# Narrow sample matmuls of a recurrent layer padded to full tiles, with elementwise work moved from VectorE to ScalarE

## The chip, the cores and the metric

One core of a Trainium2 chip runs the whole program. The metric is device time in microseconds (us); several executions are made and their median counts. The kernel before takes 676.6 us (three runs, 675.25 to 676.72).

## The reference

Two decoder layers are applied, one after the other, to a prompt of 512 tokens and to a sample group of 8 sequences with 4 new tokens each (32 tokens); the model is 1024 wide and everything is fp32.

Layer 0 projects the normalized input once into attention heads (q, k, v, gate) and convolution channels. Each of 8 heads attends within blocks; the softmax that the change touches is

```python
s = jnp.concatenate([s_sel.reshape(shp[:-2] + (n_sel,)), s_own], axis=-1)
p = jax.nn.softmax(s, axis=-1)
```

A depthwise convolution of length 31 runs beside it, and both go through one output projection.

Layer 1 is a gated linear recurrence with a 128x128 state for each of 8 heads. In chunks it computes

```python
o_inter = jnp.einsum('bhtk,bhkv->bhtv', qc * jnp.exp(b), S)
a = jnp.einsum('bhtk,bhsk,bhtsk->bhts', qc, kc, decay)
o = o_inter + jnp.einsum('bhts,bhsv->bhtv', a, vc)
S = (jnp.exp(b_last)[..., None] * S
     + jnp.einsum('bhsk,bhsv->bhkv', kc * jnp.exp(b_last[:, :, None, :] - b), vc))
```

For the samples each of the 8 sequences has its own state `S0` of 128x128 in each head, which is read, used for the 4 new tokens, updated and written back. After it come a normalization for each head, a gate and the output projection.

## The kernel before, in words

Activations lie transposed: features on the 128 partitions, 544 tokens (512 prompt, 32 sample) along the free axis, in two halves of 272 columns. A projection is a `unit`: eight blocks of the contraction times three matmuls 128x128 by 272 columns (lines 142 to 144; weights and activations are split into a high and a low fp32r part, and three of the four products are taken). The result lies in one of three PSUM buffers tagged `g`; ScalarE or VectorE evicts it. A weight tile is loaded by SyncE's queue (line 130), its high part is made on ScalarE (line 133), its low part on VectorE (line 134). Smaller PSUM buffers are tagged `s` (two), `t` (two) and `o` (one).

Layer 0: `prep` projects q, k, v and the gate of a pair of heads, `attend` takes a block of 128 queries at a time. For each of its two heads a score matmul (lines 470 and 472) fills a buffer, VectorE takes the maximum (478), ScalarE scales it (479) and computes the exponential with its sum (481), VectorE takes the reciprocal (482) and multiplies the 128 to 512 columns by it (483), TensorE transposes the result (line 102, the helper `transpose`), ScalarE copies it out (488), and TensorE multiplies by v (493). There are 32 such steps. Between them VectorE works through the convolution, 120 multiply-adds of 512 columns (line 516).

Layer 1: `proj` projects one head, `scan` runs its recurrence. The change lies in the last third of `scan`. There, for each head: `kk` is transposed (line 102), copied to `ktk` by VectorE (879) and, for the samples, to `kts` by the helper `rep4` (line 704); line 885 multiplies for the prompt's state, which VectorE chains (888, 890); lines 898 and 900 form the prompt's output. The samples' output `pos` is the sum of two matmuls, `as_` by `vs` at line 904 (32 rows by 32 columns of the array) and a selection matrix by `c4` at line 912 (128 rows by 32 columns); between them line 908 multiplies the sample queries by the states, in four column tiles 32 wide, and line 911 copies to `c4`. Line 918 forms the states' update in two halves of 512 columns, and eight VectorE instructions (line 921) scale the old states and add it. Then squares and sums on ScalarE (929, 931), the scaled output on VectorE (935, and 937 for the samples' 32 rows, tile `ons`), five transposes (four of `on` and a 32-row one of `ons`, all at line 102) and the gate (945).

The code gives dependencies, buffers and a few priorities; the order on each engine is made when the program is built, by a scheduler that simulates a timeline (`schedule_with_timeline_sim=True`). It lays `proj` of the next head between the steps of `scan`. The steps of `attend` are raised by `tc.high_priority(offset=300)`. Heads 6 and 7 are run against each other by hand (`drain(s6, s7)`), and the output projection follows in two phases. ScalarE, VectorE and GpSimd carry out their instructions in that built order.

Of the kernel before, what the change touches and what calls it, by code (L numbers as in the profile page):

```python
# [19 lines left out]
TP = 512  # L20
# [11 lines left out]
C_EXP = 448  # L32
C_SEL = 456
C_SEL2 = 472
C_END = 504


def consts():
# [28 lines left out]
def hybrid_step(ctx, tc, xt_in, cache_kt, cache_v, conv_in, hgrn_in, page_table, par_in, k_norm_0,  # L67
# [110 lines left out]
    with tc.tile_pool(name="l0", bufs=1) as lp:  # L178
# [285 lines left out]
        def attend(c, rq, qT, kT, vt, ga):  # L464
            po = bank("o")
            for i in range(4):
                L = 128 * (i + 1)
                ss = [bank("s"), bank("s")]
                for hh in range(2):
                    PE.matmul(ss[hh][:, :L], qT[:, i * 128:(i + 1) * 128], kT[:, hh, 0:L], start=True, stop=False)  # L470
                for hh in range(2):
                    PE.matmul(ss[hh][:, L - 128:L], identb, causb, start=False, stop=True)  # L472
                PTs = []
                for hh in range(2):
                    rqc = rq[:, 2 * i + hh:2 * i + hh + 1]
                    s = ss[hh]
                    mx = mk(lp, "mx", [128, 4], 4)
                    V.tensor_reduce(mx[:, 0:1], s[:, :L], axis=AX.X, op=ALU.max, negate=True)  # L478
                    A.activation(mx[:, 1:2], mx[:, 0:1], AF.Copy, scale=rqc)
                    P = mk(qp, "PP", [128, 512], 3)  # L480
                    A.activation(P[:, :L], s[:, :L], AF.Exp, bias=mx[:, 1:2], scale=rqc, accum_out=mx[:, 2:3])  # L481
                    V.reciprocal(mx[:, 3:4], mx[:, 2:3])
                    V.tensor_scalar_mul(P[:, :L], P[:, :L], mx[:, 3:4])
                    pT = bank("t")
                    for j in range(i + 1):
                        transpose(pT[:, j * 128:(j + 1) * 128], P[:, j * 128:(j + 1) * 128], 128)
                    PT = mk(qp, "PT", [128, 512], 3)
                    A.activation(PT[:, :L], pT[:, :L], AF.Copy)  # L488
                    PTs.append(PT)
                for j in range(i + 1):  # L490
                    for hh in range(2):
                        r = slice(64 * hh, 64 * hh + 64)
                        PE.matmul(po[r, i * 128:(i + 1) * 128], vt[:, j, r],  # L493
                                  PTs[hh][:, j * 128:(j + 1) * 128], start=(j == 0), stop=(j == i),
                                  tile_position=(0, 64 * hh))
            mh, ml = mtile(("h", c)), mtile(("l", c))
            V.scalar_tensor_tensor(ga[:, :TP], po, 0.5, ga[:, :TP], op0=ALU.mult, op1=ALU.mult)
            split(mh[:, :TP], ml[:, :TP], ga[:, :TP])
# [164 lines left out]
    with tc.tile_pool(name="l1", bufs=1) as lp:  # L663
# [14 lines left out]
        V.tensor_tensor(lbm[:, 3], lbm[:, 1], lbm[:, 2], op=ALU.add)  # L678
        V.tensor_tensor(lbm[:, 4], lbm[:, 3], lbm[:, 1], op=ALU.subtract)
        V.tensor_scalar(lbm[:, 5], lbm[:, 4], -1.0, 1.0, op0=ALU.mult, op1=ALU.add)  # L680
        ADs, AT, ADx, QS = [], [], [], []
        for b in range(2):
            ad = lp.tile([128, 4, 32], F32, name=f"AD{b}")
            at = lp.tile([128, 4, 128], F32, name=f"AT{b}")
            as_ = lp.tile([32, 32], F32, name=f"AS{b}")
            qs = lp.tile([128, 2, TS], F32, name=f"QS{b}")
            QS.append(qs)
            for t in (ad, at, as_, qs):
                G.memset(t, 0.0)
            ADs.append(ad)  # L690
            AT.append(at)
            ADx.append(as_)
# [4 lines left out]
        def rep4(out, src, los, n, raw=None):  # L697
            r4 = mk(lp, "r4", [128, 4, TS], 2)
            G.tensor_copy(r4, src[:, TP:T].unsqueeze(1).to_broadcast([128, 4, TS]))
            pv = bank("t", 128)  # L700
            transpose(pv, r4.rearrange("p a t -> p (a t)"), 128)
            if raw is not None:
                V.tensor_copy(raw, pv[:TS])
            A.activation(out, pv, AF.Copy)
            for l in los:
                V.tensor_tensor(out[l:l + n], pv[l:l + n], out[l:l + n], op=ALU.subtract)

        def proj(hd):
# [44 lines left out]
            for i in range(4):  # L753
                transpose(pv[:, i * 128:(i + 1) * 128], vT[:, i * 128:(i + 1) * 128], 128)
            A.activation(vt, pv, AF.Copy)
            vs = mk(lp, "vs", [TS, 128], 2)
            vx = mk(lp, "vx", [128, 128], 2, F32R)
            rep4(vx, vT, (32, 96), 32, vs)
            return f, kk, qx, qq, vt, vs, vx, gg
# [1 line left out]
        def scan(hd, f, kk, qx, qq, vt, vs, vx, gg):  # L761
# [20 lines left out]
            for l in range(4):  # L782
# [1 line left out]
                V.copy_predicated(ad.rearrange("p c (g t) -> p c g t", t=4)[:, :, :, l:],  # L784
                                  m.unsqueeze(1).to_broadcast([128, 4, 8, 4 - l]),
                                  lag(pl[:, :320].rearrange("p (c x) -> p c x", c=4), l))
                V.copy_predicated(as_.rearrange("p (n g t) -> p n g t", n=1, t=4)[:, :, :, l:], m[:32].unsqueeze(1),
                                  lag(pl[:32, 320:400].unsqueeze(1), l))
            for b2 in range(2):
                A.activation(qs[:, b2].rearrange("p (j u t) -> p j u t", u=2, t=4)[:, :, b2],  # L790
# [85 lines left out]
            for c in range(4):  # L876
                transpose(pk[:, c * 128:(c + 1) * 128], kk[:, c * 128:(c + 1) * 128], 128)
            ktk = mk(lp, "ktk", [128, 512], 1)
            V.tensor_copy(ktk, pk)
            kts = mk(lp, "kts", [128, 128], 2, F32R)  # L880
            rep4(kts, kk, (64,), 64)

            psu = bank("t")
# [16 lines left out]
                    PE.matmul(po[:, sl], qq[:, sl], S[:, (c - 1) * 128:c * 128], start=False, stop=True)  # L900
            S0 = mk(lp, "S0", [128, NS, 128], 2)
            SP.dma_start(S0, hgrn_in[hd])
            pos = bank("s", 128)[:TS]
            PE.matmul(pos, as_, vs, start=True, stop=False)
            p4 = bank("t", 128)
            for b2 in range(2):
                for j in range(4):
                    PE.matmul(p4[32 * j:32 * j + 32, :], qs[:, b2], S0[:, 2 * j + b2], start=(b2 == 0), stop=(b2 == 1),
                              tile_position=(0, 32 * j))
            c4 = mk(lp, "c4", [128, 128], 2)  # L910
            A.activation(c4, p4, AF.Copy)
            PE.matmul(pos, cst[:, C_SEL2:C_SEL2 + 32], c4, start=False, stop=True)
            ve = mk(lp, "ve", [128, NS, 128], 1, F32R)
            G.tensor_tensor(ve, vx.unsqueeze(1).to_broadcast([128, NS, 128]),  # L914
                            exm.unsqueeze(2).to_broadcast([128, NS, 128]), op=ALU.mult)
            for g in range(2):
                pn = bank("t")
                PE.matmul(pn, kts, ve[:, 4 * g:4 * g + 4, :].rearrange("p n v -> p (n v)"), start=True, stop=True)  # L918
                for n4 in range(4):
                    n = 4 * g + n4  # L920
                    V.scalar_tensor_tensor(S0[:, n, :], S0[:, n, :], tots[:, n:n + 1], pn[:, n4 * 128:(n4 + 1) * 128],  # L921
                                           op0=ALU.mult, op1=ALU.add)
            SP.dma_start(hgrns_out[hd], S0)
            yield

            sq = mk(lp, "sq", [128, 128], 2)
            sd = mk(lp, "sd", [128, 24], 2)
            G.memset(sd, 1.0)
            A.activation(sq[:TS], pos, AF.Square, accum_out=sd[:TS, 4:5])
            for c in range(4):  # L930
                A.activation(sq, po[:, c * 128:(c + 1) * 128], AF.Square, accum_out=sd[:, c:c + 1])
            rsqrt(sd[:, 8:13], sd[:, 0:5], sd[:, 16:21], 1.0 / 128, V)
            on = mk(lp, "on", [128, 4, 128], 1)
            ons = mk(lp, "ons", [TS, 128], 2)
            V.tensor_tensor(on, po.rearrange("p (c v) -> p c v", c=4), sd[:, 8:12].unsqueeze(2).to_broadcast([128, 4, 128]),
                            op=ALU.mult)
            V.tensor_scalar(ons, pos, sd[:TS, 12:13], None, op0=ALU.mult)
            gn = mk(lp, "gn", [128, T], 1)
            pk = bank("t")
            for c in range(4):  # L940
                transpose(pk[:, c * 128:(c + 1) * 128], on[:, c], 128)
            pks = bank("t", TS)
            transpose(pks, ons, TS)
            for p, sl in ((pk[:, :256], slice(0, 256)), (pk[:, 256:], slice(256, TP)), (pks, slice(TP, T))):
                V.scalar_tensor_tensor(gn[:, sl], p, vec("on"), gg[:, sl], op0=ALU.mult, op1=ALU.mult)
            for sl in (slice(0, 256), slice(256, T)):
                split(oh[hd][:, sl], ol[hd][:, sl], gn[:, sl])
# [82 lines left out]
```

## Time and profile before

| what | value |
|---|---|
| median of three runs | 676.6 us |
| the profiled execution's own time | 673.57 us |
| its span, first to last instruction | 670.7 us |
| mean granted TensorE clock | 0.991 |
| TensorE busy, share of the span | 96% |
| VectorE busy | 81% |
| ScalarE busy | 47% |
| GpSimd busy | 10% |

In the profile PE is TensorE's matmul side and PEld its weight loads, which run beside the matmuls; DVE is VectorE, ACT is ScalarE, POOL is GpSimd. "L912" is line 912. A matmul's duration in the profile runs from its issue to the end of its drain and overlaps the next one's, so what a matmul costs a busy TensorE is the step from its start to the next one's start. A shape such as 128\*32 ahead of a matmul's operands is the part of the array that it uses, rows by columns. The profiled execution lies 3.0 us under the median, and 2.9 us of its time lie around the span.

### The profile page before, as it was taken

To read this page: it belongs to the slowest core of one execution; us is meant where nothing else is said; L and a number is where in the kernel's file an instruction comes from. 1 tells how busy PE (TensorE), PEld (TensorE's weight loads), DVE (VectorE), ACT (ScalarE), POOL (GpSimd) and SP (SyncE) were. 2 spreads that over 40 slices of the span, in tenths; PEclk is the share of its full clock that TensorE was granted. 3 is DMA by queue.
4 is the path that set the end of the run, shared out by engine and by line. 5 is a ranking of instruction groups with operands and counts; after the bars stand their busy time and mean duration, and the time that the engine had idled before them with its cause. 6 is when DMAs were issued, how large, how long until landed. Compare 5 with 4: busy or idle time off the path is not lost.

```text
span 670.7 us, 14828 instructions
## 1 busy us (share of the span) xinstructions
PE 646.7 (96%) x5806; PEld 583.2 (87%) x5806; DVE 541.8 (81%) x1326; ACT 313.8 (47%) x760; POOL 70.1 (10%) x93
## 2 busy tenths in 40 slices
PE   8899999988998999999989999999999999999997
PEld 7799999966877976659989999899989989899997
DVE  6999999899967975646978977878787878777676
ACT  7332444625656867434665435443434343344221
POOL 6000110000111100000001210211011202020100
PEclk9899999989999999999999999999999999999999
DMA  9422343122120151674552232232223222222114
GB/s 254 166 80 64 98 144 108 59 70 63 50 80 31 65 175 41 222 268 143 161 162 93 70 95 100 75 119 80 97 86 122 71 100 81 97 76 83 54 56 145
DMA packets 34583, 70.51 MB, mean 105 GB/s; under 512 B 7378, under 2 KB 16210, under 8 KB 34514
## 3 DMA queue, kind: packets, MB, share of 16 engines
q1 hardware_dynamic: 34514, 69.58, 32.5%
q8 instruction: 45, 0.74, 0.4%
q14 instruction: 24, 0.20, 0.1%
HBM read 59.84 MB, written 9.73 MB: 104 GB/s over the span
## 4 chain that ended last, share of the span: by engine, by line
PE 88%; DVE 6%; DMA 2%; ACT 2%; issue 1%; SPq 1%; DVEq 0%
PE g L142 23%; PE g L144 22%; PE g L143 22%; PE t L102 4%; PE s L470 3%; DVE m L516 2%; PE o L493 2%; PE s L622 1%; PE s L779 1%; PE t L885 1%; DVE wl L134 1%; PE o L898 1%; PE o L900 1%; DMA kn<-in_cache_kt_dram 1%; DMA wr<-in_w_in_dram 1%
## 5 line engine op out<-in xcount | busy, mean ns | idle before, releaser
L142 PE MATMUL g<-h,wh 128*128 128x272 f32 x944 | 277.5, 294 | 9.3 <-ACT ga L247 3.8
L143 PE MATMUL g<-h,wh 128*128 128x272 f32 x944 | 275.6, 292 | 1.7 <-DVE h L273 1.7
L144 PE MATMUL g<-h,wl 128*128 128x272 f32 x944 | 276.0, 293 | 0.0
L142 PEld LDWEIGHTS g<-h,wh 128*128 128x128 f32 x944 | 179.4, 190 | 13.6 <-ACT ga L247 4.5
L143 PEld LDWEIGHTS g<-h,wh 128*128 128x128 f32 x944 | 179.2, 190 | 4.0 <-DVE h L273 2.1
L144 PEld LDWEIGHTS g<-h,wl 128*128 128x128 f32 x944 | 179.3, 190 | 2.0 <-issue 1.2
L133 ACT ACTIVATE wh<-wr 128x1024 fp32r<-128x1024 f32 (+4 forms) x90 | 88.2, 982 | 106.3 <-PE g L143 94.1
L134 DVE TENSOR_TENSOR wl<-wr,wh 128x1024 fp32r<-128x1024 f32 (+4 forms) x90 | 101.0, 1123 | 25.5 <-ACT wh L133 25.2
L516 DVE SCALAR_TENSOR_TENSOR m<-m,vecs,m 128x512 f32<-128x512 f32 x120 | 84.1, 735 | 0.0
L143 PE MATMUL g<-m,wh 128*128 128x272 f32 x256 | 74.2, 292 | 0.0
L144 PE MATMUL g<-m,wl 128*128 128x272 f32 x256 | 73.8, 291 | 0.0
L142 PE MATMUL g<-m,wh 128*128 128x272 f32 x256 | 73.5, 295 | 0.0
L142 PEld LDWEIGHTS g<-m,wh 128*128 128x128 f32 x256 | 47.3, 188 | 6.0 <-issue 3.6
L143 PEld LDWEIGHTS g<-m,wh 128*128 128x128 f32 x256 | 48.2, 188 | 2.5 <-issue 1.0
L144 PEld LDWEIGHTS g<-m,wl 128*128 128x128 f32 x256 | 48.1, 188 | 0.3 <-issue 0.2
L470 PE MATMUL s<-kz,qT 128*128 128x128 f32 (+3 forms) x64 | 23.7, 454 | 1.2 <-ACT PP L481 1.2
L921 DVE SCALAR_TENSOR_TENSOR S<-S,tot,t 128x128 f32<-128x128 f32 x64 | 17.6, 341 | 6.2 <-PE t L918 6.1
L488 ACT ACTIVATE PT<-t 128x128 f32<-128x128 f32 (+3 forms) x32 | 13.8, 434 | 18.7 <-PE t L102 18.7
L478 DVE TENSOR_REDUCE mx<-s 128x1 f32<-128x128 f32 (+3 forms) x32 | 15.4, 482 | 7.6 <-PE s L472 7.1
L863 DVE TENSOR_TENSOR kk<-kk,tot 128x256 f32<-128x256 f32 (+1 forms) x48 | 20.0, 417 | 0.0
L481 ACT ACTIVATE PP<-s,mx,rq 128x128 f32<-128x128 f32 (+3 forms) x32 | 19.7, 616 | 0.5
L914 POOL TENSOR_TENSOR ve<-vx,cst 128x1024 fp32r<-128x1024 f32 x8 | 15.9, 1985 | 37.5 <-PE t L918 17.7
(289 smaller groups left out, 973.0 us busy)
## 6 DMA issues: line engine op xcount, KB each, us to landing
wr<-in_w_in_dram SPq DMA_DIRECT2D x58, 512.0 KB, 3.6
wr<-in_w_out_dram SPq DMA_DIRECT2D x16, 512.0 KB, 3.6
kn<-in_cache_kt_dram SPq DMA_DIRECT2D x16, 256.0 KB, 3.4
kn<-in_cache_v_dram SPq DMA_DIRECT2D x16, 256.0 KB, 3.8
S<-in_hgrn_dram SPq DMA_DIRECT2D x8, 512.0 KB, 3.6
out_hgrns_dram<-S SPq DMA_DIRECT2D x8, 512.0 KB, 2.6
xTall<-in_xt_dram SPq DMA_DIRECT2D x8, 272.0 KB, 5.6
out_y_dram<-xTall SPq DMA_DIRECT2D x8, 272.0 KB, 2.4
```

Of the source, the lines that this page charges most:

```text
L102: PE.transpose(out, in_, ident[:np_, :np_])
L133: A.activation(wh, raw, AF.Copy)
L134: V.tensor_tensor(wl, raw, wh, op=ALU.subtract)
L142: PE.matmul(ps, wh[:, k - k0, :], ah, start=(k == k0), stop=False)
L143: PE.matmul(ps, wh[:, k - k0, :], al, start=False, stop=False)
L144: PE.matmul(ps, wl[:, k - k0, :], ah, start=False, stop=(k == k1 - 1))
L470: PE.matmul(ss[hh][:, :L], qT[:, i * 128:(i + 1) * 128], kT[:, hh, 0:L], start=True, stop=False)
L481: A.activation(P[:, :L], s[:, :L], AF.Exp, bias=mx[:, 1:2], scale=rqc, accum_out=mx[:, 2:3])
L516: V.scalar_tensor_tensor(cy[c][:, :TP], up[c][:, j:j + TP], cw[:, c, j:j + 1], cy[c][:, :TP], op0=ALU.mult, op1=ALU.add)
L863: V.tensor_tensor(k3[:, :, 0, :], k3[:, :, 0, :], t3[:, :, 1:2].to_broadcast([128, nblk, hsz]), op=ALU.mult)
L914: G.tensor_tensor(ve, vx.unsqueeze(1).to_broadcast([128, NS, 128]), exm.unsqueeze(2).to_broadcast([128, NS, 128]), op=ALU.mult)
L921: V.scalar_tensor_tensor(S0[:, n, :], S0[:, n, :], tots[:, n:n + 1], pn[:, n4 * 128:(n4 + 1) * 128], op0=ALU.mult, op1=ALU.add)
```

## The change

The 32x32 tile `AS` and the 32-row tile `vs` become 128x128 tiles that hold zeros beyond the 32 used rows and columns; the selection matrix is widened by 96 zero columns (so the constants grow from 504 to 600 columns); `ons` gets 128 rows. The matmuls at lines 904 and 912 and the fifth transpose thereby use the full array. The samples' states are scaled in place on ScalarE, in eight instructions of 128 columns, and VectorE adds the update in two instructions of 512 columns in place of eight of 128. `ktk` is copied by ScalarE. The buffers of `kts`, `c4` and `ons` go from two to one. In layer 0 the multiplication by the softmax's reciprocal (line 483) goes from VectorE to ScalarE.

```diff
-C_END = 504
+C_END = 600
...
                     V.reciprocal(mx[:, 3:4], mx[:, 2:3])
-                    V.tensor_scalar_mul(P[:, :L], P[:, :L], mx[:, 3:4])
+                    A.activation(P[:, :L], P[:, :L], AF.Copy, scale=mx[:, 3:4])
...
-            as_ = lp.tile([32, 32], F32, name=f"AS{b}")
+            as_ = lp.tile([128, 128], F32, name=f"AS{b}")
+            vs = lp.tile([128, 128], F32, name=f"VS{b}")
+            VS.append(vs)
...
-            for t in (ad, at, as_, qs):
+            for t in (ad, at, as_, qs, vs):
                 G.memset(t, 0.0)
...
-                V.tensor_copy(raw, pv[:TS])
+                V.tensor_copy(raw[:TS], pv[:TS])
...
-            vs = mk(lp, "vs", [TS, 128], 2)
+            vs = VS[hd % 2]
...
-            V.tensor_copy(ktk, pk)
-            kts = mk(lp, "kts", [128, 128], 2, F32R)
+            A.activation(ktk, pk, AF.Copy)
+            kts = mk(lp, "kts", [128, 128], 1, F32R)
...
-            pos = bank("s", 128)[:TS]
+            pos = bank("s", 128)
             PE.matmul(pos, as_, vs, start=True, stop=False)
...
-            c4 = mk(lp, "c4", [128, 128], 2)
+            c4 = mk(lp, "c4", [128, 128], 1)
             A.activation(c4, p4, AF.Copy)
-            PE.matmul(pos, cst[:, C_SEL2:C_SEL2 + 32], c4, start=False, stop=True)
+            PE.matmul(pos, cst[:, C_SEL2:C_SEL2 + 128], c4, start=False, stop=True)
+            for n in range(NS):
+                A.activation(S0[:, n], S0[:, n], AF.Copy, scale=tots[:, n:n + 1])
...
-                for n4 in range(4):
-                    n = 4 * g + n4
-                    V.scalar_tensor_tensor(S0[:, n, :], S0[:, n, :], tots[:, n:n + 1], pn[:, n4 * 128:(n4 + 1) * 128],
-                                           op0=ALU.mult, op1=ALU.add)
+                V.tensor_tensor(S0[:, 4 * g:4 * g + 4], S0[:, 4 * g:4 * g + 4], pn.rearrange("p (n v) -> p n v", n=4),
+                                op=ALU.add)
...
-            A.activation(sq[:TS], pos, AF.Square, accum_out=sd[:TS, 4:5])
+            A.activation(sq, pos, AF.Square, accum_out=sd[:, 4:5])
...
-            ons = mk(lp, "ons", [TS, 128], 2)
+            ons = mk(lp, "ons", [128, 128], 1)
...
-            V.tensor_scalar(ons, pos, sd[:TS, 12:13], None, op0=ALU.mult)
+            V.tensor_scalar(ons, pos, sd[:, 12:13], None, op0=ALU.mult)
...
-            pks = bank("t", TS)
-            transpose(pks, ons, TS)
-            for p, sl in ((pk[:, :256], slice(0, 256)), (pk[:, 256:], slice(256, TP)), (pks, slice(TP, T))):
+            pks = bank("t", 128)
+            transpose(pks, ons, 128)
+            for p, sl in ((pk[:, :256], slice(0, 256)), (pk[:, 256:], slice(256, TP)), (pks[:, :TS], slice(TP, T))):
```

## Rows read from the trace of the kernel before

**Rows 1.** page, part 1: busy us (share of the span) xinstructions

```profile
PE 646.7 (96%) x5806; PEld 583.2 (87%) x5806; DVE 541.8 (81%) x1326; ACT 313.8 (47%) x760; POOL 70.1 (10%) x93
```

**Rows 2.** page, part 4: the chain that ended last, by engine

```profile
PE 88%; DVE 6%; DMA 2%; ACT 2%; issue 1%; SPq 1%; DVEq 0%
```

**Rows 3.** stretches: us, busy PE, PEld, DVE, ACT, POOL, PEclk, DMA share, GB/s

```profile
118.00:205.00 87.00, 79.27 (x572) 68.00 (x571) 76.96 (x157) 45.59 (x103) 5.16 (x2) 0.98 0.20 62
205.00:266.00 61.00, 58.04 (x449) 47.45 (x448) 49.48 (x116) 44.89 (x105) 5.27 (x7) 1.00 0.23 75
350.00:670.00 320.00, 316.85 (x3296) 294.56 (x3296) 249.54 (x760) 127.97 (x374) 38.73 (x46) 0.99 0.28 91
```

**Rows 4.** waits of PE from 350 us on: total us, times, longest

```profile
PE g L142 <- ACT f L713: 2.6, 1, 2.6
```

**Rows 5.** timeline of PE around L912: start us, us, engine line op xcount

```profile
433.00 0.39 PE L898 MATMUL o<-vt,AT 128*128 128x128 f32 x2
433.23 0.39 PE L900 MATMUL o<-S,qq 128*128 128x128 f32 x2
433.54 0.41 PE L912 MATMUL s<-c,cst 128*32 128x128 f32 x2
433.88 0.73 PE L918 MATMUL t<-ve,kts 128*128 128x512 f32 x2
```

**Rows 6.** timeline of PE around L904

```profile
457.20 0.40 PE L904 MATMUL s<-vs,AS 32*32 32x128 f32 x2
...
457.76 0.29 PE L143 MATMUL g<-h,wh 128*128 128x272 f32 x1
```

**Rows 7.** timeline of PE around the transpose of ons

```profile
412.75 0.60 PE L102 MATMUL t<-cst,on 128*128 128x128 f32 x4
413.28 0.24 PE L102 MATMUL t<-cst,ons 32*128 32x32 f32 x1
...
413.68 0.29 PE L143 MATMUL g<-h,wh 128*128 128x272 f32 x1
```

**Rows 8.** timeline of PE, from a full transpose into a unit

```profile
424.61 0.27 PE L102 MATMUL t<-cst,r 128*128 128x128 f32 x1
...
424.85 0.29 PE L144 MATMUL g<-h,wl 128*128 128x272 f32 x1
```

**Rows 9.** weight loads by shape: xcount, busy us, mean ns, idle us before

```profile
L898 PEld LDWEIGHTS o<-vt,AT 128*128 128x128 f32 x64 | 9.2, 191 | 0.0
...
L912 PEld LDWEIGHTS s<-c,cst 128*32 128x32 f32 x16 | 1.1, 108 | 1.0
```

**Rows 10.** VectorE after 370 us, the same columns

```profile
L921 DVE SCALAR_TENSOR_TENSOR S<-S,tot,t 128x128 f32<-128x128 f32 x64 | 17.6, 341 | 6.2 <-PE t L918 6.1
...
L935 DVE TENSOR_TENSOR on<-o,sd 128x512 f32<-128x512 f32 x8 | 5.5, 692 | 0.3
```

**Rows 11.** ScalarE from 100 to 270 us, operations with a scale per partition

```profile
L479 ACT ACTIVATE mx<-mx,rq 128x1 f32<-128x1 f32 x32 | 9.0, 287 | 6.9 <-DVE mx L478 6.7
...
L436 ACT ACTIVATE kz<-t,gq 64x512 f32<-64x512 f32 x8 | 5.4, 679 | 3.9 <-PE t L102 3.8
```

**Rows 12.** L483 in two stretches: us, VectorE's busy us (count)

```profile
118.00:205.00 87.00, 6.20 (x17) 0.98 0.20 62
205.00:266.00 61.00, 6.87 (x15) 1.00 0.23 75
```

**Rows 13.** waits of PE, 100 to 270 us: total us, times, longest

```profile
PE g L142 <- ACT ga L247: 3.8, 2, 2.5
PE o L493 <- ACT PT L488: 1.5, 3, 0.7
...
PE t L102 <- DVE ksT L437: 1.3, 1, 1.3
PE s L470 <- ACT PP L481: 1.2, 3, 0.6
```

**Rows 14.** page, part 5: the convolution's multiply-adds

```profile
L516 DVE SCALAR_TENSOR_TENSOR m<-m,vecs,m 128x512 f32<-128x512 f32 x120 | 84.1, 735 | 0.0
```

More of the change, by code (lines that the diff above doesn't have):

```diff
@@ L680, in hybrid_step @@
         V.tensor_scalar(lbm[:, 5], lbm[:, 4], -1.0, 1.0, op0=ALU.mult, op1=ALU.add)
-        ADs, AT, ADx, QS = [], [], [], []
+        ADs, AT, ADx, QS, VS = [], [], [], [], []
         for b in range(2):
@@ L786, in scan @@
                                   lag(pl[:, :320].rearrange("p (c x) -> p c x", c=4), l))
-                V.copy_predicated(as_.rearrange("p (n g t) -> p n g t", n=1, t=4)[:, :, :, l:], m[:32].unsqueeze(1),
+                V.copy_predicated(as_[:TS, :TS].rearrange("p (n g t) -> p n g t", n=1, t=4)[:, :, :, l:], m[:32].unsqueeze(1),
                                   lag(pl[:32, 320:400].unsqueeze(1), l))
```

## The prediction

> **What bounds the kernel now.** I read four views in this order. The busy shares [rows 1] make TensorE the candidate: 646.7 of 670.7 us. A busy share can hide waits, so the chain that ended last comes next [rows 2]: 88% of it is TensorE, 6% VectorE, 2% ScalarE. Then the stretches [rows 3]: from 350 us on (layer 1) TensorE is busy in 316.85 of 320 us, while VectorE has 249.54 and ScalarE 127.97; from 118 to 205 us (attention beside the convolution) TensorE has 79.27 of 87 us and VectorE 76.96. Last, TensorE's own waits. In the whole of layer 1 there is one that the view lists, 2.6 us at the start, for ScalarE's L713 [rows 4]. So in layer 1 a us taken from VectorE buys nothing, and a us of TensorE's own time buys a us. In layer 0 TensorE waits now and then for either of the other two [rows 13].
>
> **Layer 1, the padded matmuls.** These are the only TensorE instructions that change, and a matmul costs the step from start to start. A pair of full-size fp32 matmuls takes 0.23 us to the next pair (L898 at 433.00, L900 at 433.23) [rows 5]. Into the 32-column pair of L912 the step is 433.54 - 433.23 = 0.31, and out of it into L918 433.88 - 433.54 = 0.34 [rows 5]. Changing the shape of the array in use thus costs 0.08 going in and 0.11 coming out, 0.19 together. The reverse way is the padding: all three groups get the full shape of the work behind them.
>
> L904, the 32x32 pair: from its start to the second matmul of the unit behind it, 457.76 - 457.20 = 0.56 us [rows 6]. I count to the second, because the first one's weights also come late. A full-size transpose takes 424.85 - 424.61 = 0.24 to the same place [rows 8], and a pair has one more step of half of 0.23, so padded it is 0.24 + 0.115 = 0.355, and 0.205 is saved. What stands before it is left out of the sum: where that is a full-size matmul another 0.08 would go.
>
> The transpose of `ons`: the four of `on` begin at 412.75, in steps of half of 0.23, so the last begins at about 413.08; `ons` follows at 413.28 and the second matmul behind it at 413.68 [rows 7]. From the last `on` that is 0.60; padded it is 0.115 + 0.24 = 0.355, and 0.245 is saved.
>
> Sum: 0.19 + 0.205 + 0.245 = 0.64 us in each head, **5.1 us in eight**, all of it in a stretch where TensorE does not wait. The cost side is the weight load: 108 ns for 32 columns, 191 ns for 128 [rows 9], two loads each at L904 and L912. I take nothing for it, since the loads of 191 ns at L898 already stand in the pairs of 0.23 us; if all of it came onto the path it would be 4 x 8 x 0.083 = 2.7 us, and that is one end of the range.
>
> **Layer 1, the work that moves.** VectorE gives up 64 instructions of 0.341 us and gets 16 of about 0.692 (the nearest row, 128x512 from PSUM) [rows 10]: 21.8 - 11.1 = 10.7 us less, and a `t` buffer is held for 0.69 in place of 4 x 0.341 = 1.36 us. TensorE waits for neither now, so the gain is nothing. ScalarE gets 64 scalings of 128 columns. It has no such row; with a scale per partition one column takes 0.287 and 512 take 0.679 [rows 11], which makes 0.38 for 128, 24.6 us in all; `ktk` adds 8 x 0.68 = 5.4 at most. ScalarE goes from 128 to about 158 of 320 us [rows 3]. The cover is its idle 162 us. If that is gone at one place, a burst of 8 x 0.38 = 3.1 us stands in a head ahead of the evictions of `g`, the high weight parts and the squares of L931, and TensorE waits for a `g` buffer; three of them stand against that. The scalings wait for the reads of L908, but `c4` ahead of them on ScalarE already waits for those, so no new wait comes ahead of the queue. `kts`, `c4` and `ons` with one buffer are written once in a head and read before the next head writes them: nothing, and where it fails, the writer waits for L918, L912 or a transpose. The larger zero fills on GpSimd run once, before the first head, and the constants' transfer on SyncE's queue grows by 49 KB, a tenth of one weight tile: nothing for both.
>
> **Layer 0, the division.** VectorE gives up 6.20 us from 118 to 205 us, where it is busy 76.96 of 87, and 6.87 us from 205 to 266 us [rows 3, 12]. ScalarE gets 32 multiplications; by its two rows 128, 256, 384 and 512 columns take 0.38, 0.48, 0.58 and 0.68, eight of each 17.0 us [rows 11], against 13.1 us before. Each step of attention grows by 0.12 us on the mean and gets one more hand-over, from the reciprocal on VectorE to ScalarE. Queued behind that wait on ScalarE are the exponential of the other head, the evictions of `prep` and the next high weight part; transposes at L102, then L488 and L493, wait for its end. The gain is bounded by VectorE's 6.20 us (TensorE is idle for 7.7 us there [rows 3]); the loss is priced below. TensorE waits for PT and PP in six places, 2.7 us, for `ga` 3.8, for `ksT` 1.3 [rows 13]: some of that will shrink with a freer VectorE and some grow with a fuller ScalarE. Between a gain of up to 6.2 and a loss of up to 12.4 I take nothing: the waits that exist are mostly behind ScalarE, which argues against the gain, and in 26 of 32 steps TensorE does not wait at all, which argues against the loss.
>
> A rule speaks against this part. The Trainium skill, "ScalarE: Activation LUTs", section "Rules for kernel authors", sends plain multiplications and additions to VectorE and not ScalarE. By that page's formula with one pointer operand an estimate for the 32 multiplications is 17.5 us, and the sum would not move. The rows agree that ScalarE is the slower of the two here (0.679 [rows 11]); what decides is the queue, in the second rival.
>
> **Sum.** The profiled execution took 673.57 us, its span 670.7; with 5.1 less it would be 668.5. It lies 3.0 us under the median, which I leave as it is: 676.6 - 5.1 = **671.5 us**.
>
> **The rivals.** *VectorE's relief counts.* In the stretch at 118 us both engines are nearly full; if TensorE's waits there shrink by all that VectorE gives up, 6.2 us, the time is 665.3. For it speaks VectorE's 88% in that stretch; against it that the largest wait, 3.8 us for `ga`, ends on ScalarE [rows 13].
>
> *ScalarE waits in line behind the convolution, and the kernel gets slower.* Place: the 17 divisions from 118 to 205 us [rows 12]. The reciprocal stands on VectorE between multiply-adds of 0.735 us [rows 14]; when it is one of them late, ScalarE stands still, and everything queued behind it does. Price: 17 x 0.73 = 12.4 us, which gives 683.9. It decides from the point where 5.1 + 1.4 = 6.5 us come through to TensorE, nine of the 17. Against it: the scheduler can lay other ScalarE work ahead of the multiplication, and ScalarE is busy only 45.59 of 87 us there [rows 3]. A few of these waits, three to eight, give 673.7 to 677.3.
>
> *The padding does not give what it says.* With the weight loads on the path the gain of layer 1 is 5.1 - 2.7 = 2.4, 674.2 us. Against it stand the pairs of 0.23 us.
>
> In the Trainium skill, "TensorE: Matmul & The Clock Gate", section "LDWEIGHTS (loading the stationary operand)", a load costs by its columns and not its rows. By its formula an estimate of this rival's price is 4 x 8 x 80 ns = 2.6 us. The rows' 108 and 191 ns agree with the difference.
>
> **How the numbers follow.** Forecast (669.5 to 673.5, which also allows a rebuilt order to add or drop some eight changes of shape elsewhere): 0.55. VectorE's relief: 0.14. A few waits on ScalarE: 0.14. Nine or more: 0.09. Weight loads: 0.08. A measurement of this kernel can tell about 0.2%, 1.4 us, from no change. Faster by more takes the forecast, the relief, the loads and a quarter of the few waits: 0.81. Within it lies the rest of the few waits: 0.10. Slower is the full queue: 0.09. The range 666 to 677 leaves out the full queue, the top of the few waits and the lowest part of the relief, some 0.15.
>
> **What would show it.** Right: L904, L912 and the `ons` transposes in shape 128\*128, with 0.23 us from the pair of L912 to L918 and 0.24 from `ons` to the second matmul behind it; TensorE's waits after 350 us still a single one of about 2.6 us; VectorE's busy time lower by about 16 us in layer 1 (10.7, and some 5 for `ktk`, by its price on ScalarE) and 13 in layer 0. Wrong: new waits of L102 or L493 for L483 on ScalarE; waits of units for evictions behind the state's scaling; steps over 0.3 us around L912; or a layer 1 that is not shorter by about 5 us from its first unit to the last instruction.

## The result, and the profile after

The changed kernel takes **670.6 us** (median of ten runs, 666.6 to 672.1) against 675.2 us for the kernel before in the same comparison: 0.9932 times, interval [0.9908, 0.9956], which is 4.6 us faster. The prediction was 671.5 us, 5.1 us faster.

The profiled execution took 672.1 us, the longest of its ten runs; that of before took 673.57 us, less than most of its own. So the two spans are nearly equal, 670.3 and 670.7 us, and can't be compared as a whole. Read in two parts they show where the time went. From the first to the last matmul of layer 1 the time falls from 316.6 to **309.6 us**. Layer 1 begins at 356.9 us instead of 349.9.

Page of the kernel after, part 1 (as in [rows 1]) and the engines' shares of the chain that ended last (as in [rows 2]):

```profile
PE 642.5 (96%) x5806; PEld 584.0 (87%) x5806; DVE 519.8 (78%) x1238; ACT 350.9 (52%) x866; POOL 67.5 (10%) x95
...
PE 87%; DVE 6%; DMA 2%; ACT 2%; issue 1%; SPq 1%; POOL 0%; DVEq 0%
```

TensorE has the same 5806 matmuls and 4.2 us less busy time. VectorE lost 22.0 us, ScalarE gained 37.1. Neither of these shows in the chain.

The stretches, columns as in [rows 3], of the kernel after; the rows from 118, 205 and 350 us answer to those:

```profile
100.00:118.00 18.00, 18.00 (x144) 17.46 (x143) 16.51 (x32) 9.16 (x22) 0.00 (x0) 1.00 0.32 104
118.00:205.00 87.00, 78.93 (x574) 68.29 (x573) 72.17 (x142) 51.77 (x115) 2.35 (x2) 0.98 0.20 62
205.00:266.00 61.00, 56.74 (x397) 46.49 (x396) 42.73 (x99) 50.37 (x118) 5.91 (x7) 0.97 0.23 75
266.00:357.00 91.00, 85.59 (x728) 68.33 (x726) 57.72 (x114) 46.88 (x93) 2.15 (x12) 0.98 0.53 177
...
350.00:670.00 320.00, 313.98 (x3329) 297.46 (x3327) 241.88 (x711) 152.76 (x452) 39.79 (x58) 0.99 0.28 93
```

and the same ahead of layer 1 in the kernel before, where the stretches between are in [rows 3]:

```profile
100.00:118.00 18.00, 18.00 (x145) 17.46 (x143) 16.47 (x32) 8.20 (x20) 0.00 (x0) 1.00 0.31 104
...
266.00:350.00 84.00, 79.98 (x677) 64.95 (x676) 56.89 (x111) 42.88 (x84) 1.68 (x10) 1.00 0.60 190
```

From 100 us to the start of layer 1 both kernels issue nearly the same matmuls: the counts of TensorE sum to 1843 in both, where one that runs across the edge of two stretches counts twice. Before, they take 250 us, of which TensorE is busy 235.3; after, 257 us, busy 239.3. The 7.0 us are 3.0 us more idle time and 4.0 us more for the same matmuls, with a granted clock of 0.97 and 0.98 from 205 us on, where it was 1.00. Between 100 and 660 us the clock fell in this execution from 2.4 to its lower level, 1.2 GHz, near 186, 217, 285 and 357 us, each time after TensorE had stood waiting; in that of before near 140 and 351 us. One of these falls in the stretches of the kernel after (columns as above):

```profile
183.00:185.00 2.00, 0.71 (x7) 0.59 (x6) 1.34 (x4) 1.36 (x2) 0.00 (x0) 1.00 0.64 244
185.00:187.00 2.00, 1.51 (x8) 1.24 (x6) 1.76 (x4) 0.40 (x1) 0.00 (x0) 0.70 0.06 19
187.00:189.00 2.00, 2.00 (x11) 2.00 (x10) 1.27 (x2) 0.00 (x0) 0.00 (x0) 0.50 0.44 120
```

TensorE is busy 0.71 of 2 us, then the clock falls to 0.50, and it is full again at half speed. The ten executions of this kernel differ in their mean granted clock, from 0.985 to 0.995, so one pair of profiles can't tell how much of the 7.0 us belongs to the change; runs price it below.

Waits of TensorE in the kernel after, first from 350 us on (as in [rows 4]), then from 100 to 350 us (as in [rows 13]): what waits, for what, total us, times, longest:

```profile
PE g L142 <- ACT f L715: 2.6, 1, 2.6
```

```profile
PE t L540 <- POOL kn L538: 2.7, 2, 2.2
PE t L102 <- ACT kz L436: 2.6, 2, 1.3
...
PE g L142 <- ACT ga L247: 1.5, 1, 1.5
...
PE t L102 <- ACT PP L483: 0.7, 2, 0.5
PE o L493 <- ACT PT L488: 0.4, 2, 0.2
```

Layer 1 has the same single wait as before. In layer 0 the wait for the division on ScalarE, L483, exists but is 0.7 us in two places; `ga` went from 3.8 to 1.5 us, PT from 1.5 to 0.4. The longest entry is new: 2.7 us at L540 for GpSimd's L538, a step of the normalization that follows the convolution.

TensorE's timeline in the kernel after at the three padded places (columns as in [rows 5]):

```profile
439.30 0.39 PE L902 MATMUL o<-S,qq 128*128 128x128 f32 x2
439.52 0.39 PE L914 MATMUL s<-c,cst 128*128 128x128 f32 x2
439.66 0.71 PE L922 MATMUL t<-ve,kts 128*128 128x512 f32 x2
```

```profile
459.53 0.45 PE L851 MATMUL s<-qq,kk 128*64 128x64 f32 x8
459.91 0.49 PE L906 MATMUL s<-VS,AS 128*128 128x128 f32 x2
460.15 0.37 PE L144 MATMUL g<-h,wl 128*128 128x272 f32 x1
460.36 0.28 PE L142 MATMUL g<-h,wh 128*128 128x272 f32 x1
```

```profile
428.84 0.39 PE L906 MATMUL s<-VS,AS 128*128 128x128 f32 x2
428.98 0.37 PE L143 MATMUL g<-h,wh 128*128 128x272 f32 x1
429.19 0.28 PE L144 MATMUL g<-h,wl 128*128 128x272 f32 x1
```

```profile
419.10 0.60 PE L102 MATMUL t<-cst,on 128*128 128x128 f32 x4
419.54 0.27 PE L102 MATMUL t<-cst,ons 128*128 128x128 f32 x1
419.56 0.37 PE L143 MATMUL g<-h,wh 128*128 128x272 f32 x1
419.78 0.28 PE L144 MATMUL g<-h,wl 128*128 128x272 f32 x1
```

Into L914 (L912 before) the step is 0.22 instead of 0.31, out of it 0.14 instead of 0.34 [rows 5]. L906 (L904 before) reaches the second matmul of the unit after 0.45 instead of 0.56 [rows 6]. `ons` begins 0.24 ahead of it instead of 0.40 [rows 7]. L906 saves least in the head at 459.91, because L851's matmuls of 64 columns stand ahead of it, as they did before: one change of shape is still there. So it is in 5 of 8 heads. In the other three its neighbour ahead is full-size, and it reaches the same place after 0.35 us (429.19 - 428.84).

The weight loads show what a change of shape does. At L912 and L918 before, then at L914 and L922 after:

```profile
433.54 0.14 PEld L912 LDWEIGHTS s<-c,cst 128*32 128x32 f32 x2
433.88 0.30 PEld L918 LDWEIGHTS t<-ve,kts 128*128 128x128 f32 x2 [0.20 <-issue]
```

```profile
439.41 0.30 PEld L914 LDWEIGHTS s<-c,cst 128*128 128x128 f32 x2
439.63 0.30 PEld L922 LDWEIGHTS t<-ve,kts 128*128 128x128 f32 x2
```

Before, each load starts together with its matmul (433.54 and 433.88). After, the load of L914 starts 0.11 us ahead of its matmul, beside the one before it. So it is all through: in layer 1 of the kernel before, the load starts within 3 ns of its matmul at each of the 169 changes of shape, and 120 ns ahead (the median) where the shape stays; in the kernel after this holds for its 117 changes too.

What ScalarE does instead, by form (columns as in [rows 10]), and VectorE's new addition:

```profile
L916 ACT ACTIVATE S<-S,tot 128x128 f32<-128x128 f32 x64 | 20.4, 390 | 4.8 <-PE t L910 4.8
```

```profile
L483 ACT ACTIVATE PP<-PP,mx 128x512 f32<-128x512 f32 x8 | 5.7, 717 | 1.1 <-DVE mx L482 1.1
L483 ACT ACTIVATE PP<-PP,mx 128x384 f32<-128x384 f32 x8 | 4.9, 613 | 0.0
L483 ACT ACTIVATE PP<-PP,mx 128x256 f32<-128x256 f32 x8 | 4.0, 507 | 2.6 <-DVE mx L482 2.6
L483 ACT ACTIVATE PP<-PP,mx 128x128 f32<-128x128 f32 x8 | 3.1, 394 | 0.3 <-DVE mx L482 0.2
```

```profile
L923 DVE TENSOR_TENSOR S<-S,t 128x512 f32<-128x512 f32 x16 | 10.5, 682 | 5.7 <-PE t L922 3.8 <-ACT sq L931 1.9
```

The durations are those that the prediction worked out (0.38 for a scaling, 0.692 for an addition and 17.0 us for all divisions; 0.390, 0.682 and 17.7 by these rows).

### The profile page after: what moved, and what is told of

It reads as the page before. It is cut to its first block, busy times and chain, and to the rows that moved or that the text cites. A ratio compares the mean times of both kernels' runs of the same rounds, so it can differ in the third digit from the quotient of the medians.

```text
span 670.3 us, 14835 instructions
## 1 busy us (share of the span) xinstructions
PE 642.5 (96%) x5806; PEld 584.0 (87%) x5806; DVE 519.8 (78%) x1238; ACT 350.9 (52%) x866; POOL 67.5 (10%) x95
## 4 chain that ended last, share of the span: by engine, by line
PE 87%; DVE 6%; DMA 2%; ACT 2%; issue 1%; SPq 1%; POOL 0%; DVEq 0%
PE g L142 23%; PE g L144 22%; PE g L143 22%; PE t L102 4%; PE s L470 2%; DVE m L516 2%; PE o L493 1%; PE s L622 1%; DMA kn<-in_cache_kt_dram 1%; PE t L887 1%; PE o L900 1%; PE s L781 1%; PE o L902 1%; PE s L587 1%; DMA xTall<-in_xt_dram 1%
## 5 line engine op out<-in xcount | busy, mean ns | idle before, releaser
L134 DVE TENSOR_TENSOR wl<-wr,wh 128x1024 fp32r<-128x1024 f32 (+4 forms) x90 | 108.0, 1201 | 37.1 <-ACT wh L133 37.0
L916 ACT ACTIVATE S<-S,tot 128x128 f32<-128x128 f32 x64 | 20.4, 390 | 4.8 <-PE t L910 4.8
L865 DVE TENSOR_TENSOR kk<-kk,tot 128x256 f32<-128x256 f32 (+1 forms) x48 | 21.8, 454 | 0.0
L918 POOL TENSOR_TENSOR ve<-vx,cst 128x1024 fp32r<-128x1024 f32 x8 | 15.5, 1942 | 62.4 <-DVE vx L708 45.5
L971 DVE TENSOR_TENSOR xTall<-g,xTall 128x272 f32<-128x272 f32 x32 | 13.4, 436 | 8.4 <-PE g L144 8.0
```

The source lines that it names most:

```text
L134: V.tensor_tensor(wl, raw, wh, op=ALU.subtract)
L865: V.tensor_tensor(k3[:, :, 0, :], k3[:, :, 0, :], t3[:, :, 1:2].to_broadcast([128, nblk, hsz]), op=ALU.mult)
L916: A.activation(S0[:, n], S0[:, n], AF.Copy, scale=tots[:, n:n + 1])
```

## The experiments

All ratios are to the kernel before in the same comparison.

**The change without the division on ScalarE, and that alone.**

```diff
-                    A.activation(P[:, :L], P[:, :L], AF.Copy, scale=mx[:, 3:4])
+                    V.tensor_scalar_mul(P[:, :L], P[:, :L], mx[:, 3:4])
```

> The kernel after with one line undone: the division of layer 0 is back on VectorE. Theory (the padding gives all of layer 1's gain, and the division on ScalarE costs layer 0 something, which the medians put at 7.1 - 4.6 = 2.5 us): the time falls to about 668 us, 7 us under the kernel before; the stretch up to the first unit of layer 1 is back at 350 us (after: 356.9), and from there to the end it stays at 313.4. Rival (the division is worth nothing, and the 7 us that layer 0 is longer in the one profile are the spread of its executions): as the kernel after, 670.6 within 1 us.

Measured: 668.65 us, 0.9897 [0.9873, 0.9921], as the theory had it. Layer 1 begins at 352.0 us and not at 350. The second kernel is the kernel before with the reverse edit.

> The kernel before with the division alone on ScalarE. Theory: 2 to 4 us slower than the kernel before; layer 1 keeps its 320.8 us from the first unit on. Rival (worth nothing): within 1 us of it.

Measured: 677.3 us, 1.0018 [1.0001, 1.0035]. That is less than the 2 to 4 us expected and hardly outside the rival's 1. The division is no gain: alone it costs 1.2 us, and taking it out of the change gains 2.4 (0.9932 - 0.9897 of 675; the intervals overlap).

**The padding alone**: the kernel after with the division, `ktk` and the states' update as they were.

> The padding alone (AS, vs, the selection matrix, ons, and the three buffers cut to one); the division, ktk and the state's update as before. Theory: 5 to 7 us faster than the kernel before, layer 1 from its first unit to the end 314 to 316 us (before 320.8), layer 0 unchanged. Rival (the wider adds and the freer VectorE give a part of layer 1's 7 us): 3 to 4 us faster, layer 1 at 317.

Measured: 671.9 us, 0.9941 [0.9919, 0.9964]: 4.0 us. Layer 1 takes 312.4 us from its first matmul to its last, 4.2 less than before. The theory's 5 to 7 us did not come; the rival's numbers did, 317.0 us from layer 1's first unit to the end: a part of its 7 us comes from the moved work. The three buffers cut to one are in it and weren't run apart; TensorE's one wait of layer 1 stayed at 2.6 us.

**The moved state work alone**: the kernel before with the scaling and `ktk` on ScalarE and the 512-wide addition, no padding.

> The moved work of layer 1 alone: states scaled on ScalarE, update added 512 wide, ktk copied by ScalarE; no padding, division as before. Theory: within 1 us of the kernel before, layer 1 from its first unit to the end at 320 to 322 us, since TensorE waits for neither engine there. Rival (it gives a part of the gain): 2 to 4 us faster, layer 1 at 317 to 319.

Measured: 673.9 us, 0.9968 [0.9955, 0.9981], 2.2 us faster; the prediction had nothing for this. Layer 1 took 315.3 us from its first matmul to its last, 1.3 less than before, but 320.9 to the end, as in the theory: behind the last matmul lie 5.3 us here and 3.8 before, a part that differs from profile to profile (3.6 to 5.2 us in kernels with the same order in layer 1). To see whether VectorE's relief is the reason, the next kernel keeps the wide addition but gives scaling and copy back to VectorE:

```diff
-            A.activation(ktk, pk, AF.Copy)
+            V.tensor_copy(ktk, pk)
...
-                A.activation(S0[:, n], S0[:, n], AF.Copy, scale=tots[:, n:n + 1])
+                V.tensor_scalar_mul(S0[:, n], S0[:, n], tots[:, n:n + 1])
```

> The state's update as in the change (scaled in place, then added 512 wide), but the scaling stays on VectorE, and ktk too: VectorE is not relieved, it gets more (in a head 8 x 0.34 + 2 x 0.69 = 4.1 us in place of 2.7). No padding, division as before. The run with the moved work alone was 2.2 us faster than before. Theory (that gain is TensorE's order, which the scheduler makes anew when the update's length changes, and not the freer VectorE): 1 to 3 us faster than the kernel before if the new order has fewer changes of the array's shape than 169 after the start of layer 1, equal or slower if it has not; TensorE still waits for VectorE nowhere in layer 1. Rival (VectorE's relief was the gain): 1 to 4 us slower than the kernel before.

Measured: 671.35 us, 0.9936 [0.9921, 0.9952], 4.3 us faster, more than the theory's 1 to 3. Its stretch of layer 1 and the only wait of TensorE there:

```profile
350.00:670.00 320.00, 314.01 (x3296) 294.35 (x3296) 254.63 (x780) 130.17 (x378) 39.19 (x56) 0.99 0.30 92
```

```profile
PE g L142 <- ACT f L713: 2.7, 1, 2.7
```

VectorE has *more* work than before (254.63 against 249.54 us [rows 3]), TensorE's wait is the same, and yet TensorE does the same 3296 matmuls in 2.84 us less. So it is not VectorE's relief. The same matmuls in another order cost TensorE less.

**`ktk` alone.**

> The copy of ktk alone on ScalarE. Theory: within 1 us of the kernel before. Rival (ktk's 5.5 us on VectorE are a part of the 2.2 us gained by the moved work): 1 us faster or more.

Measured: 675.0 us, 0.9992 [0.9977, 1.0007]: nothing.

**The order's changes of shape.** An edit can make the scheduler build a new order of TensorE's matmuls, also where it touches another engine alone, and that order sets how often two neighbouring matmuls use different parts of the array. An edit in layer 0 left layer 1 as it was: the kernel before and the one with the division alone have the same 3296 matmuls in the same order there. Counted in each trace over layer 1 (128, 64 or 32 rows and columns), beside the time from its first to its last matmul:

| kernel | changes | layer 1, us |
|---|---|---|
| before | 169 | 316.6 |
| division alone | 169 | 315.3 |
| `ktk` alone | 163 | 316.1 |
| state work alone | 160 | 315.3 |
| state work on VectorE | 148 | 313.8 |
| padding alone | 135 | 312.4 |
| after | 117 | 309.6 |
| after, division on VectorE | 117 | 309.7 |
| padding, state work on VectorE (below) | 105 | 307.5 |

From before to the last row this is 9.1 us for 64 changes, 0.14 us each. Before, 48 of the 169 changes touch L904, L912 or the transpose of `ons`, and 121 lie elsewhere. The padding leaves 5 of the 48. Elsewhere there are 130 with the padding alone, 112 after and 100 in the last row.

Two kernels with one order, before and division alone, differ by 1.3 us, and the clock is why. In the kernel before the mean granted clock is 0.72 from 350 to 356 us, behind the wait of 2.6 us that opens layer 1; the other waits as long there, but ran its layer 1 at 2.4 GHz throughout:

```profile
355.00:670.00 315.00, 315.00 (x3293) 292.77 (x3294) 248.49 (x758) 128.23 (x374) 38.87 (x46) 1.00 0.29 90
```

All other kernels of the table have one such fall there. The kernel after, that with the division on VectorE and the two half moves below share one order and one fall, and take 309.5 to 309.7 us.

The count is not the whole price. Without padding, 169 to 148 changes go at 0.14 us each; with it, 135 to 105 at 0.16. Three runs put this to the test. The first combines what was best: padding, the wide addition, and scaling, `ktk` and division all on VectorE.

> The kernel after with the division, the state's scaling and ktk all back on VectorE: padding and the 512-wide add are what is left. VectorE gets 64 x 0.34 + 8 x 0.69 = 27 us more work in layer 1 than in the kernel with only the division back. Its TensorE order as built has 105 changes of the array's shape in layer 1 (before 169, after 117). Theory (layer 1's length goes by the number of those changes, some 0.13 us each: 316.6 us from its first matmul to its last at 169, 316.1 at 163, 315.3 at 160, 313.8 at 148, 312.4 at 135, 309.6 at 117): 308.1 us in layer 1, 667 us in all, 1.5 under the kernel with only the division back. Rival (VectorE's relief was worth something): slower than that kernel, 669 to 672.

Measured: **666.8 us**, 0.9866 [0.9842, 0.9890], 9.1 us faster than before and faster than the change, with VectorE busy for 546.5 us, more than in either kernel. Layer 1 takes 307.5 us against the 308.1 expected. The second takes one scaling of 1024 columns, whose built order has 145 changes:

```diff
-            for n in range(NS):
-                A.activation(S0[:, n], S0[:, n], AF.Copy, scale=tots[:, n:n + 1])
+            V.tensor_tensor(S0, S0, tots.unsqueeze(2).to_broadcast([128, NS, 128]), op=ALU.mult)
```

> The kernel after with the division back on VectorE, and the states scaled by one VectorE instruction of 1024 columns in place of eight on ScalarE; padding as in the change. ScalarE is relieved by 20 us, and the order as built has 145 changes of shape in layer 1. Theory: layer 1 from its first matmul to its last 313.4 us, 672 us in all, 3 to 4 slower than with 117 changes, although the same matmuls run and no engine is fuller. Rival (the count does not matter, the padded shapes themselves do): 668 to 669.

Measured: 673.5 us, 0.9973 [0.9960, 0.9986], layer 1 314.5 us against the 313.4 expected. That is 0.7 us more than the kernel without padding and 148 changes takes, so kinds of changes differ in price. The third is the best kernel with the small matmuls of line 779 and the sample's one at 781 raised in priority, so that the order spreads them between unit matmuls: the same instructions, 297 changes. (Line 779 of the kernel before is 781 in the best kernel and 782 in this one.)

```diff
+            with tc.high_priority(offset=50):
+                for c in range(4):
+                    for j in range(4):
...
+                        PE.matmul(pl[32 * j:32 * j + 32, c * 80:c * 80 + 80], kk[:, t0:t0 + 32], qx[:, t0 // 32],
+                                  start=True, stop=True, tile_position=(0, 32 * j))
```

> As e9, with the small matmuls of line 779 raised in priority by 50, so that the scheduler spreads them among the units: 297 changes of shape in layer 1 in place of 105, the same instructions. Theory at 0.13 us a change: layer 1 some 25 us longer than in e9 (333 us). Rival (a change costs nothing by itself): within 2 us of e9.

Measured: 705.45 us, 1.0450 [1.0425, 1.0476], 38.6 us over the best kernel; layer 1 takes 346.7 us. TensorE's only wait in layer 1 is the same 2.6 us. The page's part 1 of the best kernel, then of this one, and a piece of its TensorE timeline:

```profile
PE 639.2 (96%) x5806; PEld 584.6 (88%) x5806; DVE 546.5 (82%) x1342; ACT 314.0 (47%) x760; POOL 67.0 (10%) x95
```

```profile
PE 678.6 (97%) x5806; PEld 599.2 (85%) x5806; DVE 547.3 (78%) x1342; ACT 312.2 (44%) x760; POOL 70.3 (10%) x95
```

```profile
400.00 0.33 PE L782 MATMUL s<-qx,kk 128*32 128x80 f32 x2
400.25 0.39 PE L144 MATMUL g<-h,wl 128*128 128x272 f32 x1
400.57 0.33 PE L782 MATMUL s<-qx,kk 128*32 128x80 f32 x2
400.83 0.39 PE L142 MATMUL g<-h,wh 128*128 128x272 f32 x1
```

The instructions are equal in number on every engine. TensorE's busy time grew by 39.4 us and its weight loads' by 14.6; the other engines' changed by less than 4. Between full-size neighbours a unit matmul steps 0.125; here one and its two small ones take 0.57. Small ones in a row cost little: in the best kernel twelve take 0.40 us to the next matmul (two take 0.25 here), so each further one costs 0.015.

```profile
368.89 0.47 PE L781 MATMUL s<-qx,kk 128*32 128x80 f32 x12
369.29 0.44 PE L102 MATMUL t<-cst,vT 128*128 128x128 f32 x2
```

That leaves 0.57 - 0.125 - 2 x 0.015 = 0.415 us for the two changes, 0.21 each. Over the 192 added changes it is (346.7 - 307.5)/192 = 0.20 us each; the clock stayed at 1.00 in this layer 1, where the best kernel has the one fall. The expected size, from 0.13, was too small. The direction and the place are shown. Whether the time goes into emptying the array or into weights that aren't loaded ahead no run separates.

**Where the division costs.** The kernel after with the division on ScalarE only in the first two or, with `if c >= 2:`, only in the last two of the four pairs of heads:

```diff
+                    if c < 2:
                         A.activation(P[:, :L], P[:, :L], AF.Copy, scale=mx[:, 3:4])
+                    else:
+                        V.tensor_scalar_mul(P[:, :L], P[:, :L], mx[:, 3:4])
```

> The kernel after with the division on ScalarE only in the first two attention steps (pairs of heads 0 and 1, while the convolution fills VectorE), back on VectorE in the last two. With it on VectorE everywhere the time was 668.7, with it on ScalarE everywhere 670.6. Theory (my second rival in a mild form: ScalarE waits behind the convolution's multiply-adds): the cost lies here, 670 to 671. Rival (the cost lies in the last two steps, where little other work covers the longer chain): 668.5 to 669.

> The kernel after with the division on ScalarE only in the last two attention steps. Theory (the cost lies behind the convolution): 668.5 to 669. Rival (it lies in the last two steps): 670 to 671.

Measured: 669.5 us, 0.9914 [0.9896, 0.9932], and 669.3 us, 0.9905 [0.9882, 0.9927]. Neither is told from the other, from the kernel without the move or from the one with all of it. Last, the best kernel with the division on ScalarE, where layer 1 is the same (105 changes, 307.7 us):

> As e9, with the division of layer 0 on ScalarE: the two differ in that line alone, and layer 1 is the same. Theory (the division costs layer 0 about 2 us): 1 to 3 us slower than e9. Rival (worth nothing): within 0.7 us of e9.

Measured: 668.0 us, 0.9887 [0.9866, 0.9909]: 1.1 us behind, again a small loss, with intervals that overlap. The stretches (columns as in [rows 3]) of the best kernel, then of this one:

```profile
100.00:180.00 80.00, 72.81 (x537) 65.18 (x536) 76.28 (x152) 41.12 (x91) 0.22 (x1) 0.98 0.24 70
180.00:230.00 50.00, 46.98 (x341) 41.11 (x341) 40.81 (x85) 32.91 (x71) 10.22 (x8) 0.97 0.19 55
230.00:345.00 115.00, 112.08 (x927) 88.60 (x926) 78.92 (x173) 63.68 (x144) 0.00 (x0) 1.00 0.53 164
```

```profile
100.00:180.00 80.00, 75.28 (x561) 68.13 (x560) 76.02 (x146) 46.94 (x103) 2.28 (x2) 0.98 0.25 73
180.00:230.00 50.00, 45.07 (x321) 38.65 (x320) 33.88 (x68) 35.47 (x79) 5.98 (x8) 0.97 0.18 51
230.00:345.00 115.00, 110.46 (x908) 86.28 (x907) 73.06 (x158) 70.45 (x156) 0.00 (x0) 1.00 0.52 161
```

Up to 180 us 24 matmuls more are issued and TensorE is busy 2.47 us more, as a freer VectorE would have it. From 180 to 230 us it is 20 fewer, from 230 to 345 us 19 fewer. At 345 us the kernel is 15 matmuls behind. The lead is real in this pair and is given back.

TensorE's waits say where. In all three kernels with the whole division on ScalarE (after, division alone, this one) L540 waits 2.7 us for GpSimd's L538 and `kz` costs 2.6 us instead of 1.3, while `ga` falls from 3.8 to 1.5 and PT from 1.5 to 0.4. In their three counterparts L540 doesn't wait. Most of that wait, 2.2 us, stands between 210 and 216 us, within the stretch where the lead is lost. But the half move of the first two pairs has it too (2.0 us) and that of the last two hasn't, and their times are alike, so it isn't shown to be the cause.

## Why the prediction was right, and where two errors cancelled

The total is right (-4.6 us against -5.1), but by two terms of the sum that were wrong with opposite signs.

**The padding, 5.1 us: right in mechanism, about a fifth too large.** Alone it measures 4.0 us, 4.2 in layer 1. The places themselves give more than priced. L912 gives 0.29 us in place of 0.19 (0.09 going in and 0.20 coming out), and 0.31 when it is counted to the second matmul behind, as the prediction did elsewhere. `ons` gives about what was priced (0.26: from the last `on` at 419.10 + 3 x 0.115 = 419.44 to 419.78 is 0.34). L904 gives half in five heads (0.11 in place of 0.205): "a full-size transpose takes 0.24 to the same place" was taken from a place with full-size neighbours, and there L851 with 64 columns stands ahead. In the other three heads it gives the 0.21 that was priced and another 0.09 in front, which was left out of the sum. Over eight heads this makes 8 x 0.31 + 8 x 0.26 + 5 x 0.11 + 3 x 0.30 = 6.0 us, and the padding alone has the same steps. The step of the prediction that was off is that the rest of layer 1 stays as it is: the rebuilt order of the padding alone has 130 changes elsewhere in place of 121, and layer 1 got only 4.2 of the 6.0 us. The missing 1.8 fit nine changes of 0.2 us; no run took these away by themselves. Weight loads don't come onto the path: the pair takes 0.22 us into L914 and 0.14 out of it, so the third rival fails.

**The moved work in layer 1, "the gain is nothing": wrong.** State work alone gives 2.2 us, and on top of the padding layer 1 loses another 2.8 us (312.4 to 309.6). The reason given, that TensorE waits for neither engine, is right, for the waits did not change. What failed is the step from "no wait goes" to "no time goes". The order was rebuilt with 117 changes of shape instead of the padding's 135. The prediction allowed for "some eight changes of shape elsewhere"; against the kernel before it was 9 more with the padding alone, 9 fewer in the change and 21 fewer in the best kernel. With the places' 6.0 us and nine changes fewer the change's layer 1 is 7.0 us shorter. Of the 2.2 us of the state work alone, 9 changes explain some 1.3, which is what layer 1 lost; the other 0.9 lies outside it, no more than the interval leaves open. Of the 4.3 us with VectorE's scaling layer 1 holds 2.8; where the other 1.5 come from is open.

That a change of shape takes time agrees with the Trainium skill, "TensorEngine Tiling (Array Packing)", section "Key Properties": a change of the tiling mode, not of the tile alone, drains TensorE. The price here, 0.14 us for a change in the kernels that differ by edits and 0.20 with 297 of them, is the runs'.

**The division, "between a gain of up to 6.2 and a loss of up to 12.4 I take nothing": a loss of 1.1 to 2.4 us** in three comparisons, each near its uncertainty, all of one sign. Of the first rival (VectorE's relief) the gain up to 180 us is seen, 2.5 us of TensorE's work, and it is lost again behind. Of the second (ScalarE in line behind the convolution) little is seen: ScalarE waits for the reciprocal 3.9 us in all (the rows of L483 above), nowhere near nine multiply-adds (6.6 us), and TensorE waits 0.7 us for L483. What the prediction did not name is the new wait for GpSimd at L540, 2.7 us. The rule of the Trainium skill that the prediction weighed, plain multiplications on VectorE, gave the right sign. The 17.5 us estimated there from the Trainium skill's formula, in "ScalarE: Activation LUTs", section "What ACT_TABLE_LOAD costs", stand beside 17.7 in the rows. Which heads carry the loss, and whether it is that wait, stays open: the two half moves did not separate.

**VectorE's busy time** fell by 22.0 us over the kernel, but in the stretch of layer 1 by 7.7 us rather than 16. The stretch is fixed at 350 us, and layer 1 begins later in this execution, so work of layer 0 stands in it; from layer 1's own first matmul to the end it falls from 249.6 to 238.3 us, 11.3. The rest is a misread row: the prediction took 64 x 0.341 = 21.8 us for the old update, but these instructions overlap, and the row's busy time is 17.6 [rows 10]. The update itself went from 17.6 to 10.5 us, 7.1 less and not 10.7.

## What to carry to other kernels

Where TensorE is full and waits for nothing, count how often neighbouring matmuls differ in the part of the array they use: here a lone small matmul between full-size ones was worth padding, and small ones cost least in groups. An edit in a kernel whose order is built by a scheduler can make a new order; compare the count in the two orders, and the granted clock of the two stretches, before a gain or loss is credited to the edit itself. Work taken off an engine that nobody waits for was worth nothing by itself: the best kernel here gives VectorE more work than the kernel before.

## What was not expected of the hardware

A change of shape has no single price. 192 more of them, with the same instructions, cost 39.2 us of layer 1, 0.20 us each, and the steps around two small matmuls between unit matmuls give the same 0.21; at L912 going in and coming out cost 0.31 together, 0.15 each. In the traces the weights of the matmul behind a change start to load with that matmul (within 3 ns, at all 169 changes before), where between equal shapes they start 120 ns ahead.

And padding from 32 to 128 columns, with four times the weight columns to load, left no trace on the path: the padded pair of L914 steps on after 0.14 us, less than the 0.23 us of the pairs ahead of it.
